# Branch C's norm weights and squares: taken at the eviction of its projections instead of in a later pass over SBUF

## The chip, the cores and the metric

The kernel runs on one core of a Trainium2 chip. The metric is the device time of one execution in microseconds (us), as a median over runs. Durations inside the program come from one profiled execution; its engines are PE (matmul; PEld is its weight load), DVE (vector), ACT (scalar), POOL (GpSimd) and SP, which issues the DMAs.

## The reference

A two-layer network in fp32 over 256 context and 256 latent tokens of width 1024, as four token tiles of 128 (tiles 0 and 1 context, 2 and 3 latent). Each layer projects the normed tokens into four branches of width 256: A a gated delta rule, B differential attention, C grouped-query attention, D windowed attention. Their outputs are gated, merged and projected, and a mixture of 16 experts follows. What the change touches is the start of branch C: q has 4 heads of 64, k and v have 2, and q and k are normed by head with a learned weight:

```python
def rms_norm(x, g):
    xf = x.astype(F32)
    return (xf * lax.rsqrt(jnp.mean(xf * xf, -1, keepdims=True) + EPS) * g).astype(x.dtype)
...
        q = rms_norm(q.reshape(b_, n, HQ_C, HEAD_DIM), qk_g[0]).reshape(b_, n, HKV_C, grp, HEAD_DIM)
        k = rms_norm(k.reshape(b_, n, HKV_C, HEAD_DIM), qk_g[1])
        return q.transpose(0, 2, 3, 1, 4), k.transpose(0, 2, 1, 3), to_heads(v, HKV_C)
    ql, kl, vl = qkv(p_lat)
    ql, kl = apply_axial_rope(ql, rope), apply_axial_rope(kl, rope)
```

## The kernel before, in words

**Stages of a layer.** A string, ORDER = "PMBIV", names the first stages: P projects branch A, M makes its 32-row triangular blocks, B projects branches B, C and D (`bcd_project`, interleaved with the modulation vectors), I inverts branch A's blocks (`a_invert`), V prepares its scan. Then come A's scan, attention, gates, merge, the output projection and the experts. The stages are written one behind the other, but a scheduler places every instruction into its engine's queue by when its inputs should be ready, so I's instructions lie between B's. A queue is then served strictly in its order: an instruction that waits holds all behind it on that engine.

**bcd_project** (L832 on). Seven groups of 256 columns of the input weights are taken in turn: D q and k (two groups), C q (column 1808), C k and v (2064), B q (1040), B k (1296), B v (1552). For each group SP loads 1 MB of weights (L127); `hilo` splits it in two halves into a 12-bit part and a rest: ACT casts `wh` (L148), the rest `wl` (L149) is a subtraction on DVE for the first half and on POOL for the second. For each token tile `natural` then makes 24 matmuls (L311 to L313, three passes for fp32) into a PSUM tile `ps_n`, of which there are two, and `to` copies it out (L861), in turns on ACT and DVE, or for a latent tile that has rotary embedding and no norm, through `rope` (L914 and L916 on DVE, L918 on POOL). In layer 1 only the latent tiles need q, so C q has two tiles instead of four; k and v keep four.

**C's norm** stands behind all seven groups: for each tile ACT squares q and k out of SBUF (L887, `csq`, two buffers shared with rotary's `rope_t`), DVE sums the squares by head (L890, `c_ss`); eleven small DVE instructions make the inverse roots of all tiles (L113 to L121, `c_iv`); then for each tile DVE multiplies by them (L895), POOL multiplies q and k by their learned weights (L899: 8 instructions in layer 0, 6 in layer 1), and the two latent tiles go through `rope`.

**a_invert** (L590 on) is a long chain on DVE: products into `i_tmp` and sums (L616 to L637), two transposes (L641, L642), then PE makes `ps_y` (L655), DVE copies it to `i_YT` (L658), and PE goes on with `ps_z` (L677, L679). Behind these stand, on PE, matmuls for the gates (`ps_gate`). `modc`, `s1b` and `c_0g` (L250, L1679, L1246) are modulation vectors, `a_N` the copies of A's blocks (L666).

Of the kernel before, what the change touches and what calls it, by code (L numbers as in the profile page):

```python
# [7 lines left out]
F32 = mybir.dt.float32  # L8
# [7 lines left out]
P = 128  # L16
# [11 lines left out]
# columns of the packed constants  # L28
# [57 lines left out]
# rows of the packed per-layer vectors (each of 128 elements)  # L86
R_BMOD, R_L1G, R_L1B, R_L2G, R_L2B, R_CONV, R_C, R_CC, NROW = 0, 48, 56, 64, 72, 80, 110, 118, 126
# columns of the packed per-layer small vectors
# [3 lines left out]
class Net:  # L92
# [16 lines left out]
    def rsqrt(self, out, x, n, tag, scale=1.0, eps=EPS):  # L109
        """out[128, n] = (x * scale + eps) ** -0.5"""  # L110
# [12 lines left out]
    def wload(self, src, shape, pool=None):  # L123
        """one streamed weight tile [128, a, b]"""
        w = (pool or self.wp).tile([P, 2048], F32, tag="w", name="w")
        v = w[:, :shape[0] * shape[1]].rearrange("p (a b) -> p a b", a=shape[0])
        self.nc.sync.dma_start(v, src)  # L127
        return v

    def split(self, w, n):  # L130
        """hi/lo parts of a streamed weight tile [128, 8, n]: lists over k of [128, n]"""
# [13 lines left out]
    def hilo(self, h, x, w, j):  # L145
        """w = h + x, h of 12 bits"""
        nc = self.nc
        nc.scalar.copy(h, w)  # L148
        (nc.gpsimd if j else nc.vector).tensor_tensor(x, w, h.bitcast(F32), op=OP.subtract)  # L149
# [5 lines left out]
    def rowbcast(self, dst, col):  # L155
        """dst [128, 1024] (every partition) = the vector held as columns col [128, 8]; two vectors: in turns of 32 partitions"""
# [16 lines left out]
    def setup(self):  # L173
# [36 lines left out]
        # silu of both conditioning vectors, padded to a column tile  # L210
# [9 lines left out]
    def mod(self, l, g):  # L220
        """modulation vectors 2g and 2g+1 of layer l, as columns"""
        nc = self.nc
        ps = self.pa.tile([P, 512], F32, tag="s", name="ps_mod")
        for k in range(8):
            src = self.a["w_mod"][l, k * P:(k + 1) * P, g * 2048:(g + 1) * 2048]
            if (l, g) == (0, 0) and k % 2:
                # at the start the weights' parts lend their tiles
# [27 lines left out]
    def all_of(*gens):  # L255
        """what the generators do, in turns"""
# [10 lines left out]
    def make_h(self, src, scl, shf):  # L267
        """src [128, 4 tiles, 1024] natural -> self.hp, transposed; scl/shf[w]: [128, 8] columns"""
# [24 lines left out]
    def h_tile(self, t):  # L293
        """both parts of the activations of token tile t: lists over k of [128, 128]"""
# [5 lines left out]
    def mm_h(self, ps, wh, wl, n0):  # L300
        """ps [128, 512 - n0] = weights.T @ activations of the tokens from n0 on"""
# [5 lines left out]
    def mm3(self, ps, lh, ll, rh, rl, nk=8):  # L307
        """ps = sum over k of (lh+ll).T @ (rh+rl), in three passes"""
# [7 lines left out]
    def a_inputs(self, l, st):  # L316
        """the projections for the decays, natural"""
# [9 lines left out]
        # the transposed keys' tile serves as scratch  # L327
# [8 lines left out]
    def a_project(self, l, st):  # L336
        """short convolution over q, k, v"""
# [5 lines left out]
        # natural k, v [tok, t, (h d)]; q is needed for a while only  # L343
# [4 lines left out]
        # transposed: [d, h, tok]  # L348
# [5 lines left out]
        def conv_tile(ci, hi, lo, c0):  # L354
            n0 = 256 if (ci < 2 and l == 1) else 0       # queries of the context are not needed
# [18 lines left out]
            # twice the silu; the factor is taken out where the result is scaled  # L374
# [19 lines left out]
        # l2 norms (of twice the silu)  # L394
# [23 lines left out]
    def a_gates(self, l, st):  # L418
        """log decays, their cumulative sums and the factors made of them"""
# [4 lines left out]
        # tiles that are filled later on serve as scratch  # L424
        Nm = A["N"] = pl.tile([P, 32, 64], F32, name="a_N")       # stack = (t, d, h)
# [16 lines left out]
        # log1p(e) = 2 atanh(s), s = e / (2 + e) <= 1/3  # L442
# [14 lines left out]
        # half of beta, for v carries a factor of two; beta itself for k  # L457
# [4 lines left out]
        # cumulative sums along the chunks, in the order of each scan: rows (head), tokens along the row;  # L462
        # the backward scan's tokens are reversed within their tile
# [11 lines left out]
        # G and G_last - G  # L475
# [10 lines left out]
        # as columns: [tok, (G, G_last - G), t, (d h)]  # L486
# [13 lines left out]
        # exp(G_last) on the partitions of the state: [d, (dir, chunk in the scan's tiles), h]  # L500
# [7 lines left out]
        # the backward rows once more, in the order of the tokens  # L508
# [6 lines left out]
        # exp(G), exp(G_last - G); beta exp(G)  # L515
# [13 lines left out]
    def a_mats(self, l, st):  # L529
        """per chunk: -(beta k k^T decay) (lower triangles) and (q k^T decay)^T"""  # L530
# [6 lines left out]
        pT = A["pT"] = pl.tile([P, 8 * nq, 64], F32, name="a_pT")      # stack = (query tile, d, h)  # L537
        nb = p1.tile([P, 4, 8], F32, name="a_nb")
        nc.vector.tensor_scalar_mul(nb, bt.rearrange("p t d h -> p t (d h)"), -1.0)
        for t in range(4):  # L540
# [16 lines left out]
            # row of -beta for the backward direction  # L557
# [27 lines left out]
    def a_invert(self, l, st):  # L585
        """R[s, c] = ((I - N)^-1)^T for the forward direction, (I - N)^-1 for the backward one"""
# [9 lines left out]
        # one 32 x 32 block per partition: F[(rb, s), j, i] = N[i, j]  # L596
        F = p1.tile([P, 32, 32], F32, tag="i_F", name="i_F")
        nc.vector.transpose(F, Dg.rearrange("p s j -> p j s"))
        T = p1.tile([P, 32, 32], F32, name="i_T")          # T[r, k], row-major
# [6 lines left out]
        def view(ap, off, dims):  # L606
            """ap: [128, n] flat; dims: (step, count)"""
# [3 lines left out]
        for r in range(1, 16):  # L611
            # rows 16 b + r, b = 0, 1
            i0 = view(Ff, r, [(16 * 33, 2), (0, r), (32, r)])                 # N[16b+r, 16b+q]  (b, k, q)
            i1 = view(Tf, 0, [(16 * 33, 2), (1, r), (32, r)])                 # T[16b+q, 16b+k]
# [3 lines left out]
        # T21 = T22 N21 T11 for the halves of 16  # L618
        Y = p1.tile([P, 16, 16], F32, name="i_Y")          # Y[j, i] = (T22 N21)[i, j]
        for i0, ni, nm in ((0, 8, 8), (8, 4, 16), (12, 4, 16)):  # L620
            # (i, j, m): T[16+i, 16+m] * N[16+m, j]
# [6 lines left out]
        for k0, nk in ((0, 8), (8, 8)):  # L628
            # (i, k, j): Y[i, j] * T[j, k], j >= k0
# [8 lines left out]
        # back: Tn[(rb, r), s, k] = T[r, k]; Rn[(rb, k), s, r] = T[r, k]  # L638
# [4 lines left out]
        # R takes N's place: first the halves of 32, from N21, then the blocks on the diagonal  # L643
        R = A["R"] = Nm
        R5 = R.rearrange("p (t d h) n -> p t d h n", t=4, d=2)
        # YT = N21^T R22, then R12 = T11^T YT (forward), T21 = YT^T T11 (backward)
# [38 lines left out]
    def a_vb(self, l, st):  # L685
        """what the scan's steps take, in their order: at step i, the chunk of each half of the partitions"""
# [19 lines left out]
    def a_scan(self, l):  # L706
        """the recurrence over chunks, both directions side by side"""
# [5 lines left out]
        for i in range(8):  # L713
# [43 lines left out]
            if outp:  # L757
# [5 lines left out]
                # the output takes the place of this step's values  # L763
# [8 lines left out]
    def a_gate_silu(self, l):  # L772
        """silu(gate) * norm weight"""
# [27 lines left out]
    def head_norm(self, pool, o, nt, mul):  # L801
        """rms norm over each head's 64 elements of o [128, nt, 256], then * mul"""
# [12 lines left out]
    def to_oT(self, pool, pp, tag, br, o):  # L815
        """natural branch output [128, nt, 256] -> transposed, to DRAM"""
# [12 lines left out]
    def bcd_project(self, l, pl):  # L829
        """natural projections [tok, cols] of the attention branches, with rotary embedding and C's norms"""  # L830
# [7 lines left out]
        B["q"] = bq = pl.tile([P, nq, 256], F32, name="b_q")         # h m d  # L838
# [24 lines left out]

        def both(f, g):
            def h(t, ps):
                f(t, ps)
                g(t, ps)
            return h

        for g in ((2320, to(dqk, 0, 256, 0, 4, 64), True),  # L870
                  (2576, both(to(dqk, 256, 128, 0, 2, 64), to(dv, 0, 128, 128, 0, 0))),
                  (1808, to(cqk, 0, 256, 0, 0, 0), True),
                  (2064, both(to(cqk, 256, 128, 0, 0, 0), to(cv, 0, 128, 128, 0, 0))),
# [5 lines left out]
        # C: rms norm of q and k, then rotary embedding  # L879
        sv = self.sv[l]  # L880
        ss = pl.tile([P, 4, 6], F32, name="c_ss")
        iv = pl.tile([P, 4, 6], F32, name="c_iv")
# [870 lines left out]
```

## Time and profile before

| | us |
|---|---|
| median of 3 runs | 2188.01 (2185.98 to 2192.87) |
| span of the profiled execution | 2171.3 |
| PE busy in it | 1849.2 (85%) |
| DVE busy | 955.9 (44%) |
| ACT busy | 503.8 (23%) |
| POOL busy | 350.6 (16%) |

The profiled execution's own time is given as its span, first to last instruction on the core; the runs' times contain what lies around that too, and their median is 16.7 us longer than the span. In the rows below "x4" is a count of instructions, "[2.15 <-POOL c_qk L899]" is idle time of the engine ahead of the row and whose result ended it, and PEclk is the granted TensorE clock, as a share of full speed.

### The profile page before, as it was taken

To read this page: it belongs to the slowest core of one execution; us is meant where nothing else is said; L and a number is where in the kernel's file an instruction comes from. 1 tells how busy PE (TensorE), PEld (TensorE's weight loads), DVE (VectorE), ACT (ScalarE), POOL (GpSimd) and SP (SyncE) were. 2 spreads that over 40 slices of the span, in tenths; PEclk is the share of its full clock that TensorE was granted. 3 is DMA by queue.
4 is the path that set the end of the run, shared out by engine and by line. 5 is a ranking of instruction groups with operands and counts; after the bars stand their busy time and mean duration, and the time that the engine had idled before them with its cause. 6 is when DMAs were issued, how large, how long until landed. Compare 5 with 4: busy or idle time off the path is not lost. (4 is left out here: it accounts for less than half of the span.)

```text
span 2171.3 us, 33547 instructions
## 1 busy us (share of the span) xinstructions
PE 1849.2 (85%) x13730; PEld 1199.7 (55%) x13730; DVE 955.9 (44%) x2126; ACT 503.8 (23%) x1038; POOL 350.6 (16%) x380
## 2 busy tenths in 40 slices
PE   6898899989999899988797898899899886676665
PEld 2676778867788555322222376778889542232221
DVE  3859547773226424221121486977755430110102
ACT  2332116752222111000000332246543100000000
POOL 1151330012532000000000125330264000000000
PEclk9999999998999899999999999999999896777767
DMA  7445413117333589999999655302487899999996
GB/s 290 161 170 194 156 36 108 54 59 260 110 126 137 211 335 350 409 409 409 409 409 409 239 194 182 130 24 96 134 271 265 323 408 409 409 409 409 409 409 274
DMA packets 200181, 553.92 MB, mean 255 GB/s; under 512 B 16222, under 2 KB 83164, under 8 KB 194396
## 3 DMA queue, kind: packets, MB, share of 16 engines
q1 hardware_dynamic: 190960, 538.56, 65.6%
q10 hardware_dynamic: 9068, 13.23, 1.7%
q8 instruction: 108, 1.77, 0.3%
q14 instruction: 45, 0.37, 0.1%
HBM read 541.25 MB, written 10.49 MB: 254 GB/s over the span
## 5 line engine op out<-in xcount | busy, mean ns | idle before, releaser
L1458 PE MATMUL ps_gu<-w,xgT 128*32 128x256 f32 (+1 forms) x1632 | 241.2, 533 | 69.5 <-DMA w<-in_w_gate_e_dram 35.5
L149 POOL TENSOR_TENSOR wl<-w,wh 128x1024 fp32r<-128x1024 f32 x62 | 154.1, 2486 | 884.1 <-DMA w<-in_w_in_dram 504.2
L1458 PE MATMUL ps_gu<-we,xgT 128*32 128x256 f32 (+1 forms) x1440 | 204.1, 512 | 38.8 <-DMA we<-in_w_up_e_dram 24.3
L1458 PEld LDWEIGHTS ps_gu<-w,xgT 128*32 128x32 f32 (+1 forms) x1632 | 78.8, 134 | 212.1 <-issue 83.0
L1500 DVE TENSOR_TENSOR y<-ps_dn,g2r 32x512 f32<-32x512 f32 (+1 forms) x128 | 70.9, 554 | 259.0 <-PE ps_dn L1489 257.5
L311 PE MATMUL ps_gate<-hh,wh 128*128 128x512 f32 (+1 forms) x512 | 179.8, 351 | 0.4 <-ACT wh L148 0.4
L313 PE MATMUL ps_gate<-hh,wl 128*128 128x512 f32 (+1 forms) x512 | 179.5, 351 | 0.0
L312 PE MATMUL ps_gate<-hl,wh 128*128 128x512 f32 (+1 forms) x512 | 179.4, 350 | 0.0
L148 ACT CAST wh<-w 128x1024 fp32r<-128x1024 f32 x124 | 129.6, 1049 | 179.2 <-PE ps_gate L312 77.3
L1458 PEld LDWEIGHTS ps_gu<-we,xgT 128*32 128x32 f32 (+1 forms) x1440 | 63.1, 128 | 167.3 <-DMA we<-in_w_up_e_dram 62.1
L1489 PE MATMUL ps_dn<-w,eaT 128*32 128x256 f32 (+1 forms) x896 | 119.1, 522 | 32.5 <-DMA w<-in_w_down_e_dram 26.8
L1468 ACT ACTIVATE eth<-ps_gu 128x512 f32<-128x512 f32 (+1 forms) x32 | 15.7, 491 | 518.4 <-PE ps_gu L1458 518.4
L311 PE MATMUL ps_n<-wh,hh 128*128 128x256 f32 x400 | 116.7, 292 | 7.3 <-DVE c_v L861 3.1
L312 PE MATMUL ps_n<-wl,hh 128*128 128x256 f32 x400 | 115.8, 290 | 8.2 <-POOL wl L149 8.2
L1471 DVE SCALAR_TENSOR_TENSOR eac<-eth,ps_gu 128x512 f32<-128x512 f32 (+1 forms) x32 | 17.7, 554 | 235.1 <-PE ps_gu L1458 235.1
L149 DVE TENSOR_TENSOR wl<-w,wh 128x1024 fp32r<-128x1024 f32 x62 | 85.9, 1385 | 72.9 <-ACT wh L148 72.6
L313 PE MATMUL ps_n<-wh,hl 128*128 128x256 f32 x400 | 115.9, 290 | 0.0
L1489 PE MATMUL ps_dn<-we,eaT 128*32 128x256 f32 (+1 forms) x640 | 93.4, 512 | 15.6 <-DMA we<-in_w_down_e_dram 11.1
L311 PEld LDWEIGHTS ps_gate<-hh,wh 128*128 128x128 f32 x512 | 99.4, 194 | 11.4 <-ACT wh L148 0.8
L312 PEld LDWEIGHTS ps_gate<-hl,wh 128*128 128x128 f32 x512 | 99.2, 194 | 10.8
L313 PEld LDWEIGHTS ps_gate<-hh,wl 128*128 128x128 f32 x512 | 99.0, 193 | 10.8 <-DVE wl L149 0.2
L1470 DVE SCALAR_TENSOR_TENSOR eth<-eth,ps_gu 128x512 f32<-128x512 f32 (+1 forms) x32 | 17.7, 554 | 193.3 <-ACT eth L1468 193.3
(453 smaller groups left out, 3591.2 us busy)
## 6 DMA issues: line engine op xcount, KB each, us to landing
w<-in_w_gate_e_dram SPq DMA_DIRECT2D x75, 1024.0 KB, 13.2
w<-in_w_down_e_dram SPq DMA_DIRECT2D x72, 1024.0 KB, 12.7
w<-in_w_up_e_dram SPq DMA_DIRECT2D x62, 1024.0 KB, 13.9
we<-in_w_up_e_dram SPq DMA_DIRECT2D x120, 512.0 KB, 13.4
w<-in_w_in_dram SPq DMA_DIRECT2D x54, 1024.0 KB, 5.2
we<-in_w_down_e_dram SPq DMA_DIRECT2D x108, 512.0 KB, 14.0
we<-in_w_gate_e_dram SPq DMA_DIRECT2D x96, 512.0 KB, 13.9
w<-in_w_mod_dram SPq DMA_DIRECT2D x44, 1024.0 KB, 5.0
```

Source lines behind the costliest of these rows:

```text
L148: nc.scalar.copy(h, w)
L149: (nc.gpsimd if j else nc.vector).tensor_tensor(x, w, h.bitcast(F32), op=OP.subtract)
L311: nc.tensor.matmul(ps, lh[k], rh[k], start=(k == 0), stop=False)
L312: nc.tensor.matmul(ps, lh[k], rl[k], start=False, stop=False)
L313: nc.tensor.matmul(ps, ll[k], rh[k], start=False, stop=(k == nk - 1))
L1458: nc.tensor.matmul(ps[M * q:M * q + M, :NF], xg[e // 4][:, 2 * kk + k, e % 4, :], w[k][:, q * NF:(q + 1) * NF], start=(kk == 0 and k == 0) ...
L1468: nc.scalar.activation(th, pss[0][:, :NF], AF.Tanh, scale=0.5)
L1470: nc.vector.scalar_tensor_tensor(th, th, 1.0, pss[0][:, :NF], op0=OP.add, op1=OP.mult)
L1471: nc.vector.scalar_tensor_tensor(ac, th, 0.5, pss[1][:, :NF], op0=OP.mult, op1=OP.mult)
L1489: nc.tensor.matmul(py[M * q:M * q + M, :NF], av[:, fc % nj, fc // nj, :], w[k][:, q * NF:(q + 1) * NF], start=(fc == 0), stop=(fc == 7))
L1500: nc.vector.tensor_tensor(ys[w][32 * e4:32 * e4 + 32, q * NF:(q + 1) * NF], py[o:o + 32, :NF], g2r[o:o + 32, q * NF:(q + 1) * NF], op=OP.mult)
```

## The change

The weight and the square are taken where a C projection leaves PSUM. A new helper `normed` replaces `to` for C's q and k: ACT squares the PSUM tile (L871), DVE writes it to SBUF multiplied by the learned weight (L872) in place of a plain copy, and DVE sums the squares (L873). The sums are still of the unweighted projection. Behind the groups remain the inverse roots, the multiplication by them (now L902) and `rope` (now L917, L919 and, on POOL, L921); POOL's multiplication is gone. (Comments are gone from the changed file too; they are left out of the diff.)

```diff
+        def normed(h0, nh, s0):
+            gw = sv[:, S_QK + (64 if h0 else 0):][:, :64].unsqueeze(1).to_broadcast([P, nh, 64])
+            def f(t, ps):
+                p3 = ps[:, s0:s0 + 64 * nh].rearrange("p (h n) -> p h n", h=nh)
+                sq = self.rp.tile([P, 384], F32, tag="rope", name="csq2", bufs=2)[:, :64 * nh].rearrange("p (h n) -> p h n", h=nh)
+                nc.scalar.activation(sq, p3, AF.Square)
+                nc.vector.tensor_tensor(cqk[:, t, 64 * h0:64 * (h0 + nh)].rearrange("p (h n) -> p h n", h=nh), p3, gw, op=OP.mult)
+                nc.vector.tensor_reduce(ss[:, t, h0:h0 + nh], sq, axis=AX.X, op=OP.add)
+            return f
...
-                  (1808, to(cqk, 0, 256, 0, 0, 0), True),
-                  (2064, both(to(cqk, 256, 128, 0, 0, 0), to(cv, 0, 128, 128, 0, 0))),
+                  (1808, normed(0, 4, 0), True),
+                  (2064, both(normed(4, 2, 0), to(cv, 0, 128, 128, 0, 0))),
...
         for t in range(4):
-            h0 = 0 if t in self.qtiles else 4
-            sq = self.rp.tile([P, 384], F32, tag="rope", name="csq2", bufs=2).rearrange("p (h n) -> p h n", h=6)[:, h0:]
-            c3 = cqk[:, t].rearrange("p (h n) -> p h n", h=6)[:, h0:]
-            nc.scalar.activation(sq, c3, AF.Square)
-            if h0:
+            if t not in self.qtiles:
                 nc.vector.memset(ss[:, t, 0:4], 1.0)
-            nc.vector.tensor_reduce(ss[:, t, h0:], sq, axis=AX.X, op=OP.add)
         self.rsqrt(iv.rearrange("p t h -> p (t h)"), ss.rearrange("p t h -> p (t h)"), 24, "c", scale=1.0 / 64)
...
-            for a, b, x in ((0, 4, 0), (4, 6, 1)):
-                if a >= h0:
-                    gw = sv[:, S_QK + 64 * x:S_QK + 64 * x + 64].unsqueeze(1).to_broadcast([P, b - a, 64])
-                    nc.gpsimd.tensor_tensor(c3[:, a:b], c3[:, a:b], gw, op=OP.mult)
```

With this the scheduler also moves what it places. On DVE in layer 0, the stretch from the rotary embedding of B k to the copy of `i_YT` before the change:

```order
L916 TENSOR_TENSOR b_k<-ps_n,const 128x256
L149 TENSOR_TENSOR wl<-w,wh 128x1024
L890 TENSOR_REDUCE c_ss<-csq_2138 128x6
...
L121 SCALAR_TENSOR_TENSOR c_iv<-rs_t,rs_y 128x24
L895 TENSOR_TENSOR c_qk<-c_qk,c_iv 128x384 x4
L914 TENSOR_TENSOR rope_t<-c_qk,const 128x12x16 x3
L916 TENSOR_TENSOR c_qk<-c_qk,const 128x384
L914 TENSOR_TENSOR rope_t<-c_qk,const 128x12x16
L916 TENSOR_TENSOR c_qk<-c_qk,const 128x384
L861 COPY b_v<-ps_n 128x256
...
L658 COPY i_YT<-ps_y 32x512 x2
```

and of the change:

```order
L919 TENSOR_TENSOR b_k<-ps_n,const 128x256
L917 TENSOR_TENSOR rope_t<-c_qk,const 128x12x16 x3
L919 TENSOR_TENSOR c_qk<-c_qk,const 128x384
L917 TENSOR_TENSOR rope_t<-c_qk,const 128x12x16
L149 TENSOR_TENSOR wl<-w,wh 128x1024
L919 TENSOR_TENSOR c_qk<-c_qk,const 128x384
L861 COPY b_v<-ps_n 128x256 x2
L250 TENSOR_TENSOR modc_114<-ps_mt,vec_106 128x4x4 x2
L1682 TENSOR_SCALAR s1b<-modc_114 128x16
L1249 TENSOR_TENSOR c_0g<-vec_93,s1b 128x8
L149 TENSOR_TENSOR wl<-w,wh 128x1024
L658 COPY i_YT<-ps_y 32x512 x2
```

The four sums, the inverse roots and the four multiplications have left this stretch; the rotary embedding of C has come forward. The sums now stand one behind each weighted copy L872 at the C tiles, between the rows of the inversion; the roots stand between the copies of `a_N` (L666), and the multiplications directly before and behind the copy of `b_q`.

In layer 1 they go further up. DVE's queue at the end of the inversion (`i_Tn` and `i_Rn` are its two results, `b_k` is B's k) reads before the change

```order
L637 TENSOR_REDUCE i_T<-i_tmp 128x8x8
L1248 TENSOR_TENSOR c_10b<-c_10b,modc_114 128x8
L641 STREAM_TRANSPOSE i_Tn<-i_T 128x32x32
L642 STREAM_TRANSPOSE i_Rn<-i_T 128x32x32
L861 COPY b_k<-ps_n 128x256
L666 COPY a_N<-i_Rn 32x2x4x32
```

and of the change

```order
L121 SCALAR_TENSOR_TENSOR c_iv<-rs_t,rs_y 128x24
L641 STREAM_TRANSPOSE i_Tn<-i_T 128x32x32
L902 TENSOR_TENSOR c_qk<-c_qk,c_iv 128x128 x2
L917 TENSOR_TENSOR rope_t<-ps_n,const 128x16x8 x2
L919 TENSOR_TENSOR b_k<-ps_n,const 128x256
L902 TENSOR_TENSOR c_qk<-c_qk,c_iv 128x384 x2
L642 STREAM_TRANSPOSE i_Rn<-i_T 128x32x32
L917 TENSOR_TENSOR rope_t<-ps_n,const 128x16x8 x2
L919 TENSOR_TENSOR b_k<-ps_n,const 128x256
L917 TENSOR_TENSOR rope_t<-c_qk,const 128x12x16 x3
L919 TENSOR_TENSOR c_qk<-c_qk,const 128x384
L666 COPY a_N<-i_Rn 32x2x4x32
```

so that roots, multiplications and C's rotary embedding now lie in front of the copies of `a_N`, which PE's `ps_y` reads. On ACT in layer 0, the C k and v tiles with what each instruction waits for (names with _49 are engines, DMAHW a transfer), before the change:

```order
L861 COPY c_qk<-ps_n 128x256 [waits PE_49]
L148 CAST wh<-w 128x1024 [waits PE_49,Activation_49]
L148 CAST wh<-w 128x1024 [waits DMAHW4_49,PE_49,Pool_49]
L861 COPY c_qk<-ps_n 128x128 [waits PE_49] x3
L666 COPY a_N<-i_Tn 32x2x4x32 [waits DVE_49]
```

and of the change:

```order
L871 ACTIVATE csq_1561<-ps_n 128x256 [waits DVE_49,PE_49,Activation_49]
L148 CAST wh<-w 128x1024 [waits DMAHW4_49]
L871 ACTIVATE csq_1618<-ps_n 128x128 [waits DVE_49,PE_49,Activation_49]
L861 COPY c_v<-ps_n 128x128 [waits DVE_49]
L871 ACTIVATE csq_1648<-ps_n 128x128 [waits PE_49,Activation_49]
L871 ACTIVATE csq_1678<-ps_n 128x128 [waits DVE_49,PE_49,Activation_49]
L861 COPY c_v<-ps_n 128x128 [waits DVE_49]
```

ACT's copies there waited for PE alone; now two copies of `c_v` come to ACT and wait for DVE, which holds what stands behind them. The weighted copy L872 on DVE, in turn, waits for ACT at every tile.

PE's own order is unchanged in layer 0; in layer 1 it changes from the end of B's projections on (attention's first matmuls come earlier, matmuls of `ps_gate` later). SP's order is unchanged, and POOL only loses its multiplications.

## Rows read from the trace of the kernel before

**Rows 1.** The page: span; the chain of waits that ended last, by engine.

```profile
span 2171.3 us, 33547 instructions
...
DMA 18%; PE 8%; DVE 1%; POOL 0%; issue 0%; ACT 0%; DVEq 0%; SPq 0%; ACTq 0%
```

**Rows 2.** Waits of SP's DMA queue, whole span: us, times, longest us.

```profile
SPq L127 <- POOL wl L149: 397.8, 53, 27.3
```

**Rows 3.** Stretches: us, PE, PEld, DVE, ACT, POOL busy, PEclk, DMA share, GB/s.

```profile
163.00:217.00 54.00, 46.45 (x364) 37.47 (x357) 51.01 (x81) 13.34 (x25) 8.92 (x7) 1.00 0.56 195
217.00:244.00 27.00, 25.51 (x209) 21.48 (x208) 6.87 (x25) 5.31 (x7) 6.04 (x5) 1.00 0.69 234
1360.00:1390.00 30.00, 24.23 (x190) 22.01 (x189) 29.45 (x35) 7.98 (x11) 9.63 (x4) 0.99 0.43 141
1390.00:1420.00 30.00, 24.80 (x246) 23.94 (x246) 26.77 (x60) 11.37 (x25) 13.40 (x13) 0.95 0.22 71
1700.00:2171.00 471.00, 329.78 (x3360) 138.81 (x3360) 75.86 (x193) 23.91 (x58) 0.00 (x0) 0.77 0.97 386
```

**Rows 4.** Waits of PE, 175 to 218 us: us, times, longest us.

```profile
PE ps_n L311 <- DVE c_v L861: 2.8, 3, 1.7
```

**Rows 5.** Waits of PE, 265 to 345 us.

```profile
PE ps_z L677 <- DVE i_YT L658: 7.1, 1, 7.1
```

**Rows 6.** Waits of PE, 1400 to 1425 us.

```profile
PE ps_stk L950 <- DVE stk L947: 2.9, 1, 2.9
PE ps_z L677 <- DVE i_YT L658: 2.3, 1, 2.3
```

**Rows 7.** DVE timeline, 186 to 266 us: start, us, engine, line, op.

```profile
189.30 3.39 DVE L625 TENSOR_TENSOR i_tmp<-i_T,i_F 128x1024 f32<-128x1024 f32 x1
...
248.90 0.18 DVE L113 TENSOR_SCALAR rs_v<-c_ss 128x24 f32<-128x24 f32 x1
...
251.49 2.77 DVE L895 TENSOR_TENSOR c_qk<-c_qk,c_iv 128x384 f32<-128x384 f32 x4
256.41 1.68 DVE L914 TENSOR_TENSOR rope_t<-c_qk,const 128x192 f32<-128x192 f32 x3 [2.15 <-POOL c_qk L899]
...
261.31 2.25 DVE L1246 TENSOR_TENSOR c_0g<-vec,s1b 128x8 f32<-128x8 f32 x1
...
264.63 1.39 DVE L658 COPY i_YT<-ps_y 32x512 f32<-32x512 f32 x2
```

**Rows 8.** POOL timeline, the same stretch.

```profile
189.22 2.39 POOL L149 TENSOR_TENSOR wl<-w,wh 128x1024 fp32r<-128x1024 f32 x1 [11.17 <-ACT wh L148]
...
252.12 5.48 POOL L899 TENSOR_TENSOR c_qk<-c_qk,sv 128x256 f32<-128x256 f32 x8 [5.55 <-DVE c_qk L895]
...
261.20 2.34 POOL L149 TENSOR_TENSOR wl<-w,wh 128x1024 fp32r<-128x1024 f32 x1
```

**Rows 9.** Stretches of PE's restart in either layer; columns as in rows 3.

```profile
258.00:265.00 7.00, 0.23 (x1) 0.00 (x0) 6.90 (x11) 0.00 (x0) 4.89 (x5) 0.87 0.05 8
265.00:275.00 10.00, 9.65 (x213) 7.24 (x214) 4.09 (x12) 1.11 (x3) 0.61 (x2) 0.58 0.31 103
...
1416.00:1422.00 6.00, 1.39 (x18) 0.88 (x11) 5.97 (x7) 2.57 (x6) 4.92 (x4) 0.86 0.01 3
1422.00:1432.00 10.00, 9.43 (x224) 8.14 (x225) 7.15 (x13) 2.99 (x8) 3.41 (x5) 0.57 0.33 107
```

**Rows 10.** DVE groups, 160 to 265 us: count, busy us, mean ns, idle before.

```profile
L890 DVE TENSOR_REDUCE c_ss<-csq 128x6 f32<-128x384 f32 x4 | 2.1, 548 | 0.9 <-ACT csq L887 0.7
...
L861 DVE COPY c_v<-ps_n 128x128 f32<-128x128 f32 x4 | 1.1, 276 | 0.0
...
L861 DVE COPY c_qk<-ps_n 128x256 f32<-128x256 f32 x2 | 0.8, 416 | 0.0
...
L916 DVE TENSOR_TENSOR b_q<-ps_n,const 128x256 f32<-128x256 f32 x2 | 0.8, 412 | 0.0
```

**Rows 11.** ACT groups, the same stretch.

```profile
L887 ACT ACTIVATE csq<-c_qk 128x384 f32<-128x384 f32 x4 | 2.0, 521 | 2.3 <-POOL b_k L918 2.3
```

More of the change, by code (lines that the diff above doesn't have):

```diff
@@ L868, in both @@
             return h
+        sv = self.sv[l]
+        ss = pl.tile([P, 4, 6], F32, name="c_ss")
+        iv = pl.tile([P, 4, 6], F32, name="c_iv")
         for g in ((2320, to(dqk, 0, 256, 0, 4, 64), True),
                   (2576, both(to(dqk, 256, 128, 0, 2, 64), to(dv, 0, 128, 128, 0, 0))),
-                  (1808, to(cqk, 0, 256, 0, 0, 0), True),
-                  (2064, both(to(cqk, 256, 128, 0, 0, 0), to(cv, 0, 128, 128, 0, 0))),
+                  (1808, normed(0, 4, 0), True),
+                  (2064, both(normed(4, 2, 0), to(cv, 0, 128, 128, 0, 0))),
                   (1040, to(bq, 0, 256, 0, 8, 32, t0), True),
@@ L878, in bcd_project @@
             yield
-        sv = self.sv[l]
-        ss = pl.tile([P, 4, 6], F32, name="c_ss")
-        iv = pl.tile([P, 4, 6], F32, name="c_iv")
         for t in range(4):
-            h0 = 0 if t in self.qtiles else 4
-            sq = self.rp.tile([P, 384], F32, tag="rope", name="csq2", bufs=2).rearrange("p (h n) -> p h n", h=6)[:, h0:]
-            c3 = cqk[:, t].rearrange("p (h n) -> p h n", h=6)[:, h0:]
-            nc.scalar.activation(sq, c3, AF.Square)
-            if h0:
+            if t not in self.qtiles:
                 nc.vector.memset(ss[:, t, 0:4], 1.0)
-            nc.vector.tensor_reduce(ss[:, t, h0:], sq, axis=AX.X, op=OP.add)
         self.rsqrt(iv.rearrange("p t h -> p (t h)"), ss.rearrange("p t h -> p (t h)"), 24, "c", scale=1.0 / 64)
```

## The prediction

> **What bounds the kernel now.** I read the page first: span and chain of waits. The chain is mostly expert weights arriving by DMA, 18% [rows 1], and the stretch that ends the program has DMA at a share of 0.97 while PE works 330 of 471 us at a mean clock of 0.77 [rows 3]. So the end is a stream. That doesn't make earlier stages free: SP's queue, which issues the transfers, stands 398 us for `wl` (L149) to give weight buffers back [rows 2], and those buffers are given back as PE, POOL and DVE get through the projections. A stage that ends earlier lets the whole queue behind it start earlier; I count time won or lost by PE in the projections fully.
>
> Next I read the stretches around branch C's projections. In layer 0 the C tiles lie in 163 to 217 us: PE works 46.45 of 54, DVE 51.01, with branch A's inversion running on it. In the following 27 us DVE works only 6.87 [rows 3]. In layer 1 the two stretches of 30 us have DVE at 29.45 and 26.77: 3.8 us of slack in 60. There DVE, not PE, sets the pace.
>
> Then PE's waits. At the C tiles of layer 0 it waits 2.8 us in three pauses for copies of `c_v` on DVE [rows 4]. After the projections it waits once for 7.1 us for `i_YT` [rows 5], and layer 1 has two such waits at the same place, 2.9 and 2.3 us [rows 6].
>
> Last, DVE's and POOL's timelines ahead of `i_YT`. C's norm lies there: sums, then roots from 248.90 to 251.49, four multiplications in 2.77, a wait of 2.15 for POOL's multiplications, which take 5.48 [rows 7, 8], rotary embedding, and only at 264.63 the copy that PE waits for.
>
> **The clock.** In 258 to 265 PE worked 0.23 us; in the following 10 us, with PE busy for 9.65, the granted clock was 0.58 of 2.4 GHz on the mean. The same in layer 1: 1.39 of 6 us busy, then 0.57 [rows 9]. Mostly 1.2 GHz, then, for 8.4 and 8.6 us (twice the missing share), which costs at most 4.2 and 4.3 us of matmul work.
>
> **Layer 0, part by part.**
>
> (a) Evictions. DVE gets a weighted copy and a sum for each tile. I price the weighted copy like the rotary product out of PSUM, 0.41 for 256 columns, and like the copy of 128, 0.28; the sum by its share of 0.548, 0.37 for four heads and 0.18 for two [rows 10]. Four q tiles: 4 x 0.78 = 3.1. Four k tiles: 4 x 0.46 = 1.8. Gone are two copies of `c_qk` (0.83) and two of `c_v`, which pass to ACT (0.55). Net +3.6 on DVE. ACT's squares were there before, 0.52 each [rows 11], and take the place of copies of about that length; ACT has idle time, 13.34 busy of 54 [rows 3]: nothing. If that cover went, it would be eight squares, at most 4.2.
>
> (b) The roots (2.6) and multiplications (2.8) move ahead of `b_q`. They run into the stretch with 20 us of DVE idle; what PE can feel is `b_q`'s copy coming late, with one more PSUM tile as reserve. For (a) and (b) together PE ends B's projections 0 to 6 us later (0 if all is covered, 6 if all of (a) and most of (b) is passed on with nothing to hide them). I take **+1.5**, near the lower end, since DVE has about 3 us idle in the first stretch and PE's present pauses amount to no more than 2.8.
>
> (c) Ahead of `i_YT` DVE loses the sums (2.1 and a wait of 0.9), roots 2.6, multiplications 2.8 and the wait for POOL 2.15: 10.5 us, more than PE's whole wait of 7.1. What is late next is `ps_y` itself, `c_0g` (2.25) and a `wl` [rows 7], so I leave 1 us of wait: **-6.1**, bounds 0 and -7.1.
>
> (d) Without a pause of that size I expect the clock to stay up: **-3** of the 4.2, as part of that stretch is small matmuls that wait for copies; bounds 0 and -4.2.
>
> POOL's eight multiplications (5.48) go; POOL's `wl` can start earlier, but it waits for ACT's cast [rows 8], so nothing. SP issues the same transfers in the same order: nothing. Layer 0: 1.5 - 6.1 - 3 = **-7.6**.
>
> One row I weighed against a rule. The inversion's product L625 took 3.39 us beside POOL's `wl` from 189.22 to 191.6 [rows 7, 8], and `c_0g`, eight columns, 2.25 beside another. The weighted copy reads one operand out of PSUM, as the rotary product did, and keeps its 0.41 in my sum. The Trainium skill (SBUF — State Buffer, "Who interferes with whom") says that a DVE instruction with two SBUF inputs and a GpSimd instruction that reads SBUF exclude each other, and that one with a single SBUF input stays out of it: the two long rows agree. Were the weighted copy held like `c_0g`, two of them would meet a `wl` in this stretch and the sum would be some 4 us higher.
>
> **Layer 1.** The same by kind, with two q tiles: evictions 1.6 + 1.8 less one copy of `c_qk` and two of `c_v`, +2.4. Multiplications 2.77 scaled by columns (1024 of 1536), 1.85; roots 2.6; rotary embedding four halves of 0.56 and two products of 0.6, 3.4. These 10.2 us all stand now in front of the copies of `a_N`, and DVE has no room. PE's last projections are held by the evictions and half of the multiplications, which are ahead of `b_k`'s rotary product: +3.3 (bounds 0 and 10.2). But DVE's total hardly grows (2.4 less the old sums, 1.5, is 0.9), while the waits for squares (0.9) and for POOL (2.15 in layer 0) go: `i_YT` comes 1 us earlier (bounds +3 and -3). PE's idle 5.2 us shrinks to 5.2 - 3.3 - 1 = 0.9; PE restarts **1 us** earlier, and I take **-2.5** of the 4.3 for the clock. PE's changed order behind that, attention before gates, I set at 0, within the two waits it could save or double, about 3 either way. Layer 1: **-3.5**.
>
> **Sum:** -11.1. The working rests on an execution of 2171.3 us span; the median of the runs shown lies 16.7 above it, for what lies around the span and run to run. I add the sum to the median: 2188.0 - 11.1 = **2177 us**. Bounds of this case: all favourable, -11.3 in layer 0 and -7.3 with the earliest `i_YT` and the whole clock in layer 1, about 2169; without either clock's gain, 2183.
>
> **Rivals.**
>
> 1. *Layer 1 takes back half.* DVE's 10.2 us of moved work, less 3.05 of saved waits and the 3.8 of slack, come before `a_N`: PE restarts 3.4 us later, still after a pause, still at the lower clock. -7.6 + 3.4 = -4.2: 2184. For it: 29.45 of 30 [rows 3]. Against it: the total on DVE doesn't grow, the moved work only changes place. That is within 0.3%, about what a measurement of this kernel can tell from no change (6.6 us).
>
> 2. *The C tiles become a chain of hand-overs, and it is slower.* Each tile is now squared on ACT, then copied on DVE, then summed, and at two k tiles in each layer ACT waits for DVE again, with casts of `wh` behind it. In order on a DVE that is full, each hand-over costs up to a square (0.52) and a mean DVE instruction (51.01 us over 81, 0.63): 1.15 a tile, 9.2 us in layer 0 and 6.9 in layer 1. Less the 6.1 of (c), with both stretches at the lower clock kept because pauses only change place: +10, **2198**. It decides where PE's waits at the C tiles exceed about 1 us each; today three pauses make 2.8 [rows 4]. Against it: two PSUM tiles, and DVE instructions around the C tiles that are mostly short. The Trainium skill (PSUM — Partial Sum Buffer, "PSUM bank collisions raise a hardware error") states that two engines must not access one bank at a time, which speaks against this change: the square and the weighted copy of a tile can't overlap. The changed order agrees, every weighted copy waits for ACT; no row of before shows the price.
>
> 3. *Nothing arrives at the end.* The stream of expert weights is as full as it can be [rows 3], and an earlier start is used up by waits elsewhere: 2188. Against it: SP's waits for released buffers [rows 2].
>
> **How the numbers follow.** My forecast gets 0.60, rival 1 0.17, rival 2 0.15 and rival 3 0.08. Of the forecast some 0.04 lies above 2181.4, which is within 0.3%; of rival 1 0.02 lies below it. Faster: 0.56 + 0.02 = 0.58. Same: 0.04 + 0.15 + 0.08 = 0.27. Slower: 0.15. The range goes from 2167 (the favourable bounds, and 2 us of spread between runs, 2185.98 to the median) to 2192, which takes in rivals 1 and 3 and leaves out rival 2.
>
> **What would show it.** Right: PE's wait for `i_YT` in layer 0 at 0 to 2 us; a clock near 1.0 in the ten microseconds after it; POOL with 14 multiplications fewer; the idle pair in layer 1 together under 2 us; PE's waits at the C tiles of layer 0 below 5 us. Wrong: a new PE wait of 5 us or more in either layer before `ps_z` (rival 1, or attention's first inputs), waits of 1 us at each C tile (rival 2), or both gaps closed and the last expert's weights arriving at the same time (rival 3).

## The result, and the profile after

| | before | after |
|---|---|---|
| median, us | 2186.99 (2182.25 to 2192.87, 4 runs) | 2165.68 (2163.32 to 2168.22, 4 runs) |
| ratio, 95% interval | | 0.9917 (0.9889 to 0.9945) |
| profiled execution's span | 2171.3 | 2164.7 |

Faster, by 18 us of 2187 by the ratio (12 to 24 by its interval); 2177 was forecast, 11 us less than before, and the median lies just below the range's lower end of 2167. A second comparison, in the experiments, gave 0.9930 (0.9899 to 0.9961), 15 us. So the direction and the place were right, and the size was short by some 4 to 7 us; a gain of 11 us lies just outside the first interval and inside the second (9 to 22 us).

The two profiled executions are only 6.6 us apart. The timed execution behind the changed kernel's profile took 2166.49 with a span of 2164.7: only 1.8 us lie around a span, and my reading of 16.7 as "what lies around the span and run to run" was nearly all the second. The first profile of before was a short execution. So stretches of the program are compared below, each with the low clock in it, and not spans.

The busy stretches of the changed kernel, to be laid against [rows 3] and [rows 9] (columns as there):

```profile
163.00:217.00 54.00, 49.17 (x391) 40.23 (x388) 52.03 (x100) 13.81 (x28) 10.13 (x7) 1.00 0.64 213
217.00:244.00 27.00, 23.05 (x186) 19.65 (x185) 11.69 (x36) 5.17 (x6) 7.75 (x6) 1.00 0.59 198
244.00:265.00 21.00, 19.30 (x371) 16.94 (x369) 11.64 (x24) 4.67 (x8) 5.69 (x7) 1.00 0.33 102
265.00:275.00 10.00, 9.27 (x120) 7.15 (x119) 3.57 (x6) 3.14 (x8) 7.54 (x8) 1.00 0.08 28
```

DVE's 6.87 us of work in 217 to 244 have become 11.69: the work moved into the empty stretch. The clock behind is 1.00 where it was 0.58. PE's waits in layer 0, 155 to 300 us (us in total, times, longest), answer to [rows 4] and [rows 5]:

```profile
PE ps_mod L237 <- DMA w<-in_w_mod_dram: 6.0, 4, 2.7
PE ps_n L312 <- POOL wl L149: 1.9, 3, 0.9
PE ps_z L677 <- DVE i_YT L658: 1.7, 2, 1.0
PE ps_n L311 <- DVE c_qk L872: 1.2, 1, 1.2
...
PE ps_n L311 <- DVE b_q L861: 0.5, 1, 0.5
```

The single wait of 7.1 us is two of 1.0 and 0.7; the waits for `c_v` are gone, and 0.5 for a `b_q` copy has come. The wait for weights of the modulation, in the same stretch before the change, was shorter:

```profile
PE ps_mod L237 <- DMA w<-in_w_mod_dram: 3.3, 3, 1.6
```

DVE's timeline shows where the work went and when `i_YT` is copied (264.63 before [rows 7]):

```profile
210.31 0.17 DVE L113 TENSOR_SCALAR rs_v<-c_ss 128x24 f32<-128x24 f32 x1
...
218.09 1.03 DVE L902 TENSOR_TENSOR c_qk<-c_qk,c_iv 128x384 f32<-128x384 f32 x2
219.03 0.42 DVE L861 COPY b_q<-ps_n 128x256 f32<-128x256 f32 x1
219.37 1.02 DVE L902 TENSOR_TENSOR c_qk<-c_qk,c_iv 128x384 f32<-128x384 f32 x2
...
253.00 0.42 DVE L861 COPY b_v<-ps_n 128x256 f32<-128x256 f32 x1 [5.21 <-PE ps_n L313]
...
255.22 0.17 DVE L1249 TENSOR_TENSOR c_0g<-vec,s1b 128x8 f32<-128x8 f32 x1
255.31 1.22 DVE L149 TENSOR_TENSOR wl<-w,wh 128x1024 fp32r<-128x1024 f32 x1
256.44 1.39 DVE L658 COPY i_YT<-ps_y 32x512 f32<-32x512 f32 x2
```

Ahead of `i_YT` DVE now waits for PE, where PE waited for DVE. The vector `c_0g`, which took 2.25 us beside POOL's `wl` [rows 7, 8], takes 0.17. The costs of the new instructions, DVE by group, 160 to 262 us (count, busy us, mean ns, idle before):

```profile
L902 DVE TENSOR_TENSOR c_qk<-c_qk,c_iv 128x384 f32<-128x384 f32 x4 | 2.0, 552 | 0.0
L872 DVE TENSOR_TENSOR c_qk<-ps_n,sv 128x256 f32<-128x256 f32 x4 | 1.7, 416 | 0.0
L873 DVE TENSOR_REDUCE c_ss<-csq 128x4 f32<-128x256 f32 x4 | 1.6, 407 | 0.0
L873 DVE TENSOR_REDUCE c_ss<-csq 128x2 f32<-128x128 f32 x4 | 1.1, 276 | 0.0
L872 DVE TENSOR_TENSOR c_qk<-ps_n,sv 128x128 f32<-128x128 f32 x4 | 1.1, 275 | 0.0
```

The weighted copy costs what a copy costs, as priced, and the sums 0.41 and 0.28 us where I had 0.37 and 0.18; the multiplication by the roots takes 552 ns in place of 753, now that POOL has no multiplications beside it (before, the four took 0.56, 0.55, 1.09 and 0.81 us, and POOL's first began with the second of them). By the rule quoted in the prediction (the Trainium skill, SBUF — State Buffer, "Who interferes with whom") both are to be expected. The multiplications agree with it. These rows can't show it for the weighted copy, since no copy of layer 0 ran beside a POOL instruction here; in e9 two did, beside a `wl`, and took 0.42 us each (its rows are below).

**Stretches of all executions.** For each profiled execution, in us, from starts of PE's instructions in its timeline: A from the 301st `ps_n` matmul (in layer 0's C k and v) to the first `ps_y` (the C q tiles lie ahead of it: 15.5 us before, 16.1 after, from the 193rd `ps_n` matmul to the 289th); G from there to the scan's first `ps_u`, which holds the wait for `i_YT`; S on to attention's first `ps_stk`; in layer 1, Y from the last `ps_n` matmul to the last `ps_z`, which holds the waits of [rows 6], and Z on from there to the 37th `ps_ot` matmul, the first that takes branch A's output in layer 1. In brackets what the low clock takes of it, (1 - PEclk) x length.

| | A | G | S | Y | Z |
|---|---|---|---|---|---|
| before | 63.6 (0) | 19.1 (5.1) | 70.0 (0) | 16.4 (5.1) | 66.0 (0) |
| before again (e1) | 64.0 (0) | 19.0 (5.1) | 70.0 (0) | 16.5 (5.1) | 66.0 (0) |
| **after** | 61.3 (0) | 10.4 (0) | 69.9 (0) | 10.2 (0.1) | 74.0 (8.0) |
| after again (e8) | 63.1 (3.4) | 10.7 (0) | 70.6 (1.7) | 10.2 (0) | 69.0 (1.7) |
| e2, layer 0 alone | 61.8 (1.7) | 12.2 (3.0) | 71.0 (2.1) | 16.9 (5.3) | 71.4 (6.6) |
| e3, layer 1 alone | 63.5 (0) | 19.1 (5.1) | 70.0 (0) | 10.4 (0.3) | 74.5 (8.2) |
| e4, norm behind i_YT | 63.0 (1.7) | 10.6 (0) | 87.1 (6.8) | 16.5 (5.1) | 66.0 (0) |
| e5, squares early | 66.1 (3.4) | 10.7 (0) | 69.9 (0) | 16.3 (5.1) | 66.0 (0) |
| e6, weights early | 63.3 (1.7) | 14.8 (3.4) | 69.9 (0) | 16.4 (5.1) | 66.0 (0) |
| e7, c_v on ACT | 68.4 (5.1) | 19.7 (6.6) | 70.8 (2.0) | 16.6 (5.1) | 66.0 (0) |
| e9, copy twice | 65.8 (1.7) | 9.9 (0) | 70.2 (0) | 10.2 (0.1) | 74.0 (8.0) |
| e10, c_v on DVE | 64.4 (3.4) | 9.9 (0) | 69.9 (0) | 10.4 (0.3) | 74.1 (8.0) |

### The profile page after: what moved, and what is told of

Read it like the earlier page. It is cut to its first block, busy times and chain, and to the rows that moved or that the text cites. A ratio compares the mean times of both kernels' runs of the same rounds, so it can differ in the third digit from the quotient of the medians.

```text
span 2164.7 us, 33549 instructions
## 1 busy us (share of the span) xinstructions
PE 1849.5 (85%) x13730; PEld 1198.9 (55%) x13730; DVE 946.1 (44%) x2139; ACT 503.9 (23%) x1037; POOL 341.2 (16%) x366
## 5 line engine op out<-in xcount | busy, mean ns | idle before, releaser
L313 PEld LDWEIGHTS ps_gate<-hh,wl 128*128 128x128 f32 x512 | 99.1, 193 | 10.8 <-DVE wl L149 0.2
L312 PEld LDWEIGHTS ps_gate<-hl,wh 128*128 128x128 f32 x512 | 98.7, 193 | 10.8
```

Of the source, the lines that this page charges most:

```text
L312: nc.tensor.matmul(ps, lh[k], rl[k], start=False, stop=False)
L313: nc.tensor.matmul(ps, ll[k], rh[k], start=False, stop=(k == nk - 1))
```

## The experiments

**e1, the kernel before once more** (no edit).

> The kernel before, unchanged, once more, to place its profiled execution (span 2171.3) against its median of 2187. Theory N (its executions differ by some 13 us among themselves and the first profile was a short one): ratio 1.000, and a span of this profile between 2171 and 2190 that need not repeat 2171.3. If it repeats 2171 to 2173 while the median stays at 2187, what a profile shows and what a timed run takes differ in a way that a profile can't explain.

Ratio 1.0001 (0.9976 to 1.0026). The span is

```profile
span 2182.1 us, 33547 instructions
```

10.8 us longer than the first, and on its chip the executions of before ranged from 2169.6 to 2197.6 (33 runs). Theory N holds. The stretches above repeat to 0.4 us, so a stretch can be read from one profile where the whole span can't, if its low clock, in brackets, is laid beside it: this moves between executions of one kernel (A of the changed kernel has 0 of it in one and 3.4 us in e8).

**e2, the change in layer 0 alone; e3, in layer 1 alone.**

```diff
-                  (1808, normed(0, 4, 0), True),
+                  (1808, normed(0, 4, 0) if l == 0 else to(cqk, 0, 256, 0, 0, 0), True),
...
-                nc.gpsimd.tensor_tensor(c3[:, a:b], c3[:, a:b], gw, op=OP.mult)
+                if l != 0:
+                    nc.gpsimd.tensor_tensor(c3[:, a:b], c3[:, a:b], gw, op=OP.mult)
```

(the k and v group and the squares likewise; e3 with `l == 1`)

> The change in layer 0 alone. Theory T (the gain is layer 0's: DVE's norm work leaves the stretch ahead of i_YT, the wait of 7.1 us and the low clock behind it go, some 10.9 us in the profile, and layer 1 gives some 3 us back): 2 to 4 us faster than the whole change, near 2162, and in the profile PE's first scan matmul of layer 0 (ps_u) near 264 us after the start. Rival L (both layers gain): slower than the whole change, near 2175.

> The change in layer 1 alone. Theory T: 2 to 4 us slower than the kernel before, near 2190, with layer 0's wait of 7 us for i_YT back and, in layer 1, PE's restart earlier by 4 to 5 us but the end of attention some 3 us later. Rival L (both layers gain): near 2176.

e2: 0.9931 (0.9906 to 0.9955), 15 us faster, all of the effect within the intervals; `ps_u` at 265.7 us against 274.5 before (280.9 in e1: what lies ahead of these stretches varies too). e3: 0.9992 (0.9965 to 1.0019), nothing that can be told from zero (-8 to +4 us). In e3's table row the wait in layer 1 goes (Y 16.5 to 10.4) and 8.5 us come back behind it (Z), nearly all at the low clock. Theory T holds in that layer 0 carries the gain; that e2 beats the whole change isn't shown (0.9931 against 0.9917 and 0.9930).

**e4, layer 0's old norm, tied behind the inversion.** The old evictions and the old pass over SBUF, but its squares take a scale of 1.0 that is computed from the inversion's result, so that all of it comes behind `i_YT` (the pass itself is also written behind stage V; that part is left out here):

```diff
+            if l == 0:
+                tie = pl.tile([P, 1], F32, name="tie")
+                nc.vector.tensor_scalar(tie, self.A["N"][:, 31, 0:1], 0.0, 1.0, op0=OP.mult, op1=OP.add)
...
-                nc.scalar.activation(sq, c3, AF.Square)
+                nc.scalar.activation(sq, c3, AF.Square, scale=tie if l == 0 else 1.0)
```

> The kernel before, but in layer 0 the whole norm of branch C (squares out of SBUF, sums, roots, multiplications on DVE and POOL, rotary embedding) is tied to the end of the inversion, behind i_YT; the evictions are the old copies. Theory T: the wait for i_YT goes here too, with the clock's stretch, less a few us that the norm now takes beside the scan: 5 to 9 us faster than before, near 2180. Rival E (the gain is the eviction's: shorter holds of PSUM, no pass over SBUF, no work on POOL): no gain, 2187, or slower by what the scan loses.

1.0005 (0.9972 to 1.0038): no gain, though G fell to 10.6 as theory T had it. Both theories are half right. The norm's work does hold `i_YT`, and without it there PE's wait and the low clock are gone. But it costs as much in its new place: S grew from 70.0 to 87.1. Of these 17.1 us 8.5 come back up to the first `ps_xg`, at the start of the experts (from the first `ps_stk` 384.6 before, 376.1 in e4), for 21 more matmuls of `ps_gate` are done within S; the 8.6 that are left are what G had won (8.5). PE's waits in e4, 250 to 350 us:

```profile
PE ps_s L727 <- DVE S L755: 2.9, 1, 2.9
PE ps_ot L824 <- DVE ao L813: 2.2, 1, 2.2
PE ps_d L748 <- DVE u L743: 1.4, 1, 1.4
PE ps_z L677 <- DVE i_YT L658: 1.0, 1, 1.0
PE ps_u L737 <- DVE rs_y L121: 1.0, 1, 1.0
...
```

The scan, which goes back and forth between PE and DVE, waits for DVE instead, and a stretch at the low clock (285 to 310 us: 0.83) comes with that:

```profile
275.00:285.00 10.00, 6.64 (x62) 4.87 (x62) 7.67 (x14) 2.48 (x4) 7.79 (x9) 0.92 0.32 105
285.00:310.00 25.00, 23.54 (x254) 18.29 (x256) 14.59 (x31) 1.72 (x4) 6.74 (x8) 0.83 0.06 23
```

So the change pays because it moves the work forward, much of it into the 27 us in which DVE was nearly idle; taking it off the place where it stood is not enough by itself.

**e5, squares and sums early; e6, weights early.** Layer 0 alone, in both the change cut in half. e5 copies without weights and leaves those to POOL:

```diff
                 nc.scalar.activation(sq, p3, AF.Square)
-                nc.vector.tensor_tensor(cqk[:, t, 64 * h0:64 * (h0 + nh)].rearrange("p (h n) -> p h n", h=nh), p3, gw, op=OP.mult)
+                nc.vector.tensor_copy(cqk[:, t, 64 * h0:64 * (h0 + nh)], ps[:, s0:s0 + 64 * nh])
```

e6 keeps the weighted copy and has squares and sums in the old pass:

```diff
-                nc.scalar.activation(sq, p3, AF.Square)
                 nc.vector.tensor_tensor(cqk[:, t, 64 * h0:64 * (h0 + nh)].rearrange("p (h n) -> p h n", h=nh), p3, gw, op=OP.mult)
-                nc.vector.tensor_reduce(ss[:, t, h0:h0 + nh], sq, axis=AX.X, op=OP.add)
```

> Layer 0 alone, squares and sums at the eviction, a plain copy, and the weights still multiplied by POOL over SBUF behind the roots. Theory S (the sums are the head of the chain: once they are early, roots and multiplications, POOL's too, move into the stretch where DVE is idle): from PE's first ps_y to its first ps_u 10 to 12.5 us, against 19.1 before and 10.4 with the whole change, and a time near that of the change in layer 0 alone (ratio near 0.993). Theory G (POOL's pass over SBUF, with its wait of 2.15 us, is what held i_YT): 16 to 19 us there, and a ratio near 1.000.

> Layer 0 alone, weights at the eviction, nothing on POOL, but squares and sums in a pass over SBUF behind all projections, as before. (The squares are then of weighted values: branch C's norm in layer 0 is not the reference's.) Theory S: only POOL's wait leaves the stretch ahead of i_YT, so 16 to 18 us from the first ps_y to the first ps_u, the low clock still behind it, and a gain of 2 to 3 us there. Theory G: 10 to 12.5 us, and the whole gain.

G is 10.7 us in e5, as with the whole change, and 14.8 in e6, between the two expectations. PE's waits in e6, 240 to 275 us:

```profile
PE ps_z L677 <- DVE i_YT L658: 3.4, 1, 3.4
PE ps_n L312 <- POOL wl L149: 0.7, 1, 0.7
```

Theory S holds for the stretch: early sums are enough to bring everything forward, POOL's weights too; early weights alone halve the wait (7.1 to 3.4) and leave a stretch at the low clock that takes 3.4 us. By time, e5 is 0.9962 (0.9942 to 0.9981) and e6 0.9974 (0.9952 to 0.9997). e5's 8 us are fewer than e2's 15; the two intervals overlap, and its A (66.1) had 3.4 us of low clock, so what the weights add to the time is open. Theory S's ratio near 0.993 is not reached.

**e7, two copies of c_v on ACT, in the kernel before; e10, all four on DVE, in the changed kernel.**

```diff
-                    (nc.scalar.copy if self.flip() else nc.vector.tensor_copy)(d, s_)
+            f = self.flip()
+            if l == 0:
+                f = t % 2 == 0
+            (nc.scalar.copy if f else nc.vector.tensor_copy)(cv[:, t], ps[:, 128:256])
```

(e7, for `c_v` only; e10 with `f = 0`)

> The kernel before, with two of layer 0's four copies of c_v (tiles 0 and 2) on ACT in place of DVE, nothing else. PE's waits for c_v (2.8 us) are gone with the change. Theory V (they go because these copies left DVE's queue): the stretch from the middle of C's k and v projections (the 300th ps_n matmul) to the first ps_y falls from 63.6 to 61 to 62, and i_YT's stretch stays at 19. Theory W (they go because the weighted copy stands elsewhere in DVE's order): 63 to 64 as before. Time: within 0.2% of before by either.

> The changed kernel with all four copies of c_v of layer 0 on DVE, as before the change. Theory V (PE's waits for c_v went because two copies left DVE): they come back, 2 to 3 us, and the stretch to ps_y is longer by as much. Theory W (they went because DVE's queue is ordered anew at these tiles): waits for c_v stay under 1 us.

e7: 0.9978 (0.9958 to 0.9999). PE's waits in layer 0's projections and inversion, e7 first, e10 second:

```profile
PE ps_z L677 <- DVE i_YT L658: 7.1, 1, 7.1
...
PE ps_n L312 <- POOL wl L149: 2.8, 2, 2.1
PE ps_n L311 <- DVE c_v L868: 2.1, 1, 2.1
...
```

```profile
...
PE ps_n L311 <- DVE c_v L880: 2.8, 1, 2.8
PE ps_n L311 <- DVE c_qk L872: 1.2, 1, 1.2
PE ps_z L677 <- DVE i_YT L658: 1.0, 1, 1.0
PE ps_n L312 <- POOL wl L149: 0.7, 1, 0.7
```

In the kernel before, the move alone leaves 2.1 of the 2.8 us; in the changed one, taking it back brings 2.8 us in one wait. Neither theory holds alone: a copy of `c_v` costs PE when it stands behind long instructions of the inversion, and whether it does depends on both edits and on the rest of the queue. In e4, with the old evictions and all four copies on DVE, these waits are 0.6 us. A in e10 is 64.4, of which 3.4 are low clock, so its length settles nothing, and e7's 68.4 (5.1) neither. By time e10 is 0.9957 (0.9925 to 0.9989).

**e9, every weighted copy of layer 0 twice, in the changed kernel.**

```diff
                 nc.vector.tensor_tensor(cqk[:, t, 64 * h0:64 * (h0 + nh)].rearrange("p (h n) -> p h n", h=nh), p3, gw, op=OP.mult)
+                if l == 0:
+                    nc.vector.tensor_tensor(cqk[:, t, 64 * h0:64 * (h0 + nh)].rearrange("p (h n) -> p h n", h=nh), p3, gw, op=OP.mult)
```

> The changed kernel with every weighted copy of layer 0 made twice (eight more DVE instructions at the evictions, 2.8 us, each tile of PSUM held 0.3 to 0.4 us longer). Theory P (DVE's extra work at the evictions reaches PE, as the prediction's 1.5 of 3.6 us assumed): PE's waits for c_qk, c_v and wl in layer 0's projections grow by 1 us or more from 1.2, 0 and 0.7 to 1.9. Theory Q (PE feels only where the copy stands in DVE's queue; there is room): they grow by less than 0.5 us together, and i_YT's stretch stays at 10 to 11 us. Layer 1 is the changed one: two more samples, with the next run, of its stretch behind ps_z, 74.0, 74.5 and 69.0 so far (66.0 in six of seven with the old order).

0.9967 (0.9940 to 0.9994). PE's waits, 140 to 262 us, and rows of DVE and POOL from their timelines:

```profile
...
PE ps_n L312 <- POOL wl L149: 3.1, 2, 2.4
PE ps_n L311 <- DVE c_v L861: 2.1, 1, 2.1
PE ps_n L311 <- DVE c_qk L874: 1.9, 1, 1.9
```

```profile
190.46 2.40 POOL L149 TENSOR_TENSOR wl<-w,wh 128x1024 fp32r<-128x1024 f32 x1 [13.23 <-ACT wh L148]
191.89 0.42 DVE L874 TENSOR_TENSOR c_qk<-ps_n,sv 128x256 f32<-128x256 f32 x1
...
205.71 2.42 POOL L149 TENSOR_TENSOR wl<-w,wh 128x1024 fp32r<-128x1024 f32 x1 [12.85 <-ACT wh L148]
206.13 2.98 DVE L636 TENSOR_TENSOR i_tmp<-i_Y,i_T 128x512 f32<-128x512 f32 x1
```

7.1 us where the changed kernel has 1.9 + 1.2 = 3.1: with 2.8 us more work on DVE came 4 us more of waits. That is theory P's number. That the work as such made them isn't shown: the 2.1 us for `c_v` stand behind a product of the inversion, L636, that took 2.98 us beside POOL's `wl`, where the five others in e9 took 1.0 to 1.1, and the 2.4 us for `wl` behind a POOL `wl` of 3.5 us instead of 2.4.

**e8, the changed kernel once more** (no edit).

> The changed kernel once more. Layer 0's stretches should repeat: 61 to 62 us from the 300th ps_n to ps_y, 10 to 12 from there to ps_u. Layer 1, from the end of the inversion (last ps_z) to the last but eleventh ps_ot of branch A: if the low clock there comes with the changed order, 73 to 75 us again with some 8 us lost to it; if it comes by chance, it can be 66 to 70. Ratio 0.990 to 0.995.

0.9930 (0.9899 to 0.9961). G repeats (10.7); A has 3.4 us of low clock this time. In layer 1, Z is 69.0 with 1.7 lost; the other four executions with the changed layer 1 have 74.0 to 74.5 with 8.0 to 8.2. With the old layer 1 it is 66.0 in six of seven and 71.4 in one. So the low clock behind the inversion comes in four of five executions with the changed order and in one of seven with the old.

## Why the prediction was right, and where it was not

**(c) and (d), layer 0's wait and its clock: right, the clock not in every execution.** The forecast was -6.1 and -3; G fell from 19.1 to 10.4. PE's wait for `i_YT` went from 7.1 to 1.7, which is -5.4, and the remaining 3.3 I put down to the clock (of the 5.1 in the table 0.9 lay within the wait itself, [rows 9]). e4 shows the cause by itself, and e5 which part of the change does it: the sums at the head of the chain. With the whole change in layer 0 the clock stayed up through G in four of five executions. In e2 it fell all the same, 5.1 us over G and S, behind one wait of 1.0 us and with PE as busy as in the changed kernel. The two stretches behind the first `ps_y`, e2 first, then the changed kernel:

```profile
255.00:260.00 5.00, 3.96 (x121) 2.92 (x121) 3.92 (x11) 0.14 (x1) 0.97 (x3) 0.96 0.65 213
260.00:270.00 10.00, 10.00 (x119) 7.54 (x115) 3.05 (x6) 2.74 (x6) 3.47 (x4) 0.51 0.01 2
```

```profile
255.00:260.00 5.00, 3.96 (x136) 2.91 (x134) 3.70 (x11) 0.36 (x1) 0.90 (x4) 1.00 0.69 213
260.00:270.00 10.00, 9.34 (x164) 7.26 (x158) 3.05 (x6) 4.24 (x10) 5.22 (x6) 1.00 0.08 28
```

**(a) and (b), the projections: wrong in sign.** "For (a) and (b) together PE ends B's projections 0 to 6 us later ... I take +1.5." A became 2.3 us shorter (63.6 to 61.3, no low clock in either; e2 has 61.8 and e8 63.1, of which 1.7 and 3.4 are low clock). The term need not be free: in e9 extra work there went with 4 us more of waits. But the trace of before already held what speaks the other way: of PE's waits in [rows 4], 2.8 us were for `c_v` on DVE, and the change takes two of these copies to ACT and places all of the tile's work anew in DVE's queue. I counted the microseconds that DVE gains and not which instruction each copy stands behind. Part of what was won is lost again at the next limit: PE waits 6.0 us for weights of the modulation, 3.3 before.

**Layer 1: right in mechanism for half, its sum not borne out.** Forecast: projections 3.3 later, the pause nearly gone, -2.5 for the clock, -3.5 in all. The 3.3 did not come where I had put them, at B's tiles: the last 240 `ps_n` matmuls take 36.6 to 38.2 us with the changed layer 1 and 37.7 to 37.8 with the old. D's and C's tiles ahead of them are some 2 to 3 us longer (80.1 after, 77.0 before), which is more low clock (8.5 and 5.1); three other executions, of both kinds (e2, e6, e10), have 80.9 to 83.4 with 12 to 14 of it. The pause went: Y fell by 6.2 us, waits and 5.0 of low clock together. But Z rose by 8.0 (3.0 in e8). PE's waits behind the projections, changed kernel, 1340 to 1440 us:

```profile
...
PE ps_z L677 <- ACT stk L940: 1.3, 1, 1.3
PE ps_n L311 <- DVE b_k L919: 0.9, 1, 0.9
PE ps_stk L953 <- DVE stk L950: 0.8, 1, 0.8
...
```

and the stretches around PE's restart:

```profile
1404.00:1416.00 12.00, 9.91 (x302) 8.55 (x301) 9.43 (x16) 5.83 (x13) 6.28 (x7) 0.94 0.30 91
1416.00:1430.00 14.00, 14.00 (x92) 11.94 (x90) 6.50 (x22) 5.18 (x15) 4.19 (x6) 0.57 0.00 0
```

There is no pause of 5 us any more (1.3 and 0.8 are 2.1, where I had named under 2 as the sign), and PE was busy for 9.91 of 12 us; the clock still fell to its lower level, 0.57 on the mean of the next 14 us. My step "without a pause of that size I expect the clock to stay up" held in layer 0 in four of five executions and failed here in four of five, where what PE did was mostly 32-wide products and short waits. What exactly made it fall isn't settled. By time the net of layer 1 is -8 to +4 us (e3), which excludes neither my -3.5 nor rival 1's +3.4. In the profiles it is rival 1's number, by another way than it named (the clock, not work ahead of `a_N`): from layer 1's first `ps_n` matmul to the end of Z 197.3 us before and 200.9 after, 200.5 to 205.8 in four of five executions with the changed layer 1 (196.3 in e8) and 197.1 to 197.5 in five of seven with the old (201.4 in e6, 207.0 in e2).

**The sum.** Layer 0's A and G make -11.0 in the profile, which is the forecast's sum only because two errors cancel: 3.8 better than forecast in (a) and (b), and layer 1's 3.5 that didn't come in the profile. (A slip of the working, on which nothing hangs: without either clock's gain its terms give 2182.4, not 2183.) By time the change gives 15 to 18 us, and layer 0 alone 15 (10 to 21). Where the 4 to 7 us beyond A and G lie isn't settled: the profiles of the changed kernel have nothing of that size in one place. Some 2 us may lie in layer 0's attention and what follows it: from the first `ps_stk` to the first `ps_xg`, less the low clock, it is 363.8 to 365.4 us in the five executions with the whole change in layer 0 and 366.3 to 366.9 in the six others (e4 apart).

**Rival 2** did not come, and part of its mechanism is visible: two copies of `c_v` on ACT wait 4.8 us for DVE's weighted copy, and PE waits 1.2 us at one C tile of layer 0 and 2.4 at one of layer 1 (1.1 before), not 1.15 at each. The tile of the 1.2 us had its square done at 178.6 us; its weighted copy began at 181.7, behind a product of the inversion. So it waited for its turn on DVE and not for ACT.

```profile
L861 ACT COPY c_v<-ps_n 128x128 f32<-128x128 f32 x2 | 0.5, 266 | 4.8 <-DVE c_qk L872 4.8
```

That the two readers of a tile don't overlap (the Trainium skill, PSUM — Partial Sum Buffer, "PSUM bank collisions raise a hardware error") holds in the order; in layer 0 it costs ACT, which is busy for 13.81 of 54 us at these tiles. **Rival 3** fell: time won in layer 0 arrives at the end, with a tail as full as before (DMA share 0.97 from 1700 us on in both).

## What to carry to other kernels

Look for the wait that ends last, then for the earliest point at which the work ahead of it could run, and for an engine that is idle there; the same work moved behind the wait (e4) removed the wait and gained nothing. In a chain of small instructions it is the head that has to move: with the sums early, the scheduler brought the rest forward by itself. And read single stretches with their clock, not spans, where executions of one kernel differ by more than the effect.

## What the hardware showed that I had not expected

Executions of the unchanged kernel on one core differ by up to 28 us (2169.6 to 2197.6), and two profiles of it by 10.8, with the low clock falling into different places: between `ps_gR` and the first `ps_kk`, early in layer 0, one execution lost nothing to it and the other 3.7 us. A pause of PE of 3.4 us (e6) was followed by 3.4 us lost to the lower level of 1.2 GHz, one of 7.1 by 5.1, and pauses of 1.0 and 0.7 by none in the changed kernel. But in e2 a pause of 1.0 at the same place was followed by 5.1, waits of 2.3 to 2.9 us in layer 0's projections were followed by 1.7 in some cases (e2, e10) and by none in others (the changed kernel), and in layer 1 short pauses between small products were followed by 8.0. From the length of the pause alone it couldn't be told.
